# A float32 feed-forward down-projection by Strassen's scheme in four passes, tokens on the output's partitions

## The chip, the cores and the metric

The kernel runs on one core of a Trainium2 chip. What is measured is the device time of one execution, in microseconds (us). Five engines work side by side, each with its own queue in program order: TensorE (PE, matmuls), VectorE (DVE), ScalarE (ACT), GpSimd (POOL) and SyncE (SP, which here only starts transfers). SP, ACT and POOL each have a queue of DMA issues; all transfers share 16 DMA engines.

## The reference, cut to what matters

One layer of a streaming encoder, 512 tokens, width 2048, everything in float32: a token mixer, a cross-attention into 256 memory tokens, and a feed-forward part, each added to a residual, and a final RMSNorm. The change is about the end of it:

```python
def conv_ffn(h, w_up, conv_w, w_down):
    u = causal_dwconv(h @ w_up, conv_w)
    gate, up = u[..., :D_FF], u[..., D_FF:]
    return (jax.nn.silu(gate) * up) @ w_down
...
        x = x + conv_ffn(h, w_ffn_up[l], ffn_conv[l], w_ffn_down[l])
    return rmsnorm(x, final_norm)
```

D_FF is 5632, so the hidden matrix is 512 x 5632 and w_down is 5632 x 2048.

## The kernel before

Activations lie transposed, channels on the 128 partitions and the 512 tokens along the row. A float32 product is made of three matmuls of a rounded type: each operand is split into a high part (an ACT cast) and a low part (a DVE subtraction), and high x high, low x high and high x low are summed in PSUM (mm3, L153 to L156). Weights come in pieces of 128 x 1024 (512 KB): wpiece (L134 to L145) loads one on SP's queue into one of five buffers and splits it into one of three pairs of buffers, whi and wlo (L143, L144); raw and wsplit (L829 to L839) do the same in two steps. Small tiles of 128 x 512 come from a pool of 64 (T).

**Out-projection.** The loop at L860 makes 16 tiles of the residual: 24 matmuls each into a bank psx (out_proj), the old residual tile loaded on SP and added on DVE (L878), the sum stored to x2_d on ACT's queue (L879), its square added on POOL (L245), and after each second tile up_prepare makes, on DVE and ACT, the sums that the next stage needs.

**Up-projection.** The loop over 44 units (L953) makes a gate tile and an up tile of the hidden matrix by Strassen's scheme: seven products of 24 matmuls with 256 columns each (product, L898 to L900). pair_loads (L841) loads four weight pieces and lets two accumulating loads on POOL's queue make sums of them; the others are made on DVE. up_half (L946) and gate_half (L940) apply the norm, the convolution, Silu and the product of both, and L951 stores the tile to hid_d on ACT's queue.

**Down-projection.** The output is made transposed, four tiles of 128 channels at a time (four PSUM banks), over eleven steps of four hidden tiles. Steps run in the order of the list steps (L913): 44 of them, the last two of them held back. Each step loads four hidden tiles on POOL's queue (hid_load, L919), splits them (hid_split), loads and splits two weight pieces (w_split, two pieces ahead) and issues 48 matmuls of 512 columns; the hidden matrix is so loaded and split four times. At the end of a group the residual tile is added (L1075) and its square summed. The order on ACT, DVE and POOL is written out (manual_schedule, L1042), PE's is the scheduler's.

**End.** The last two steps run again by token halves (tail_mm, 256 columns, L1079), so that the norm of the first half can be made beside the second: rstd_rows (L231) sums squares over partitions on PE and rsqrt (L209) takes Ln and Exp on ACT and three DVE operations. out_pair (L1105) multiplies and stores on SP's queue (L1110); the host transposes the result.

## Time and profile before

| | us |
|---|---|
| median of 3 runs (2832.14 to 2836.43) | 2833.61 |
| the profiled execution | 2834.4 |
| its span, first to last instruction | 2832.6 |
| PE busy | 2806.2 |
| DVE busy | 1835.9 |
| ACT busy | 1354.3 |
| POOL busy | 351.9 |

The profile is one execution seen by the hardware profiler. Busy time of PE contains matmuls that overlap each other, so a busy share of 99% says that PE was never without one, not that it works at its peak. The duration of a matmul (0.389 us for 512 columns) is longer than the distance from one to the next. Where an engine was idle, the profile names what released it. The clock that TensorE was granted is 0.998 of full speed over the span.

### The profile page before, as it was taken

How to read it: one execution, taken by the hardware profiler on the slowest of the kernel's cores; microseconds unless marked ns; L12 is line 12 of the kernel's file. 1: busy time of each engine (PE TensorE's matmuls, PEld its weight loads, DVE VectorE, ACT ScalarE, POOL GpSimd, SP SyncE). 2: the span in 40 equal slices, each digit the busy share in tenths (PEclk: the TensorE clock that was granted, in tenths of full speed). 3: DMA queues.
4: the chain of work that ended last, by engine and by line, in shares of the span. 5: the costliest groups of instructions: out<-in, count | busy, mean ns of one | idle time of the engine just before them, and what ended most of it. 6: DMA issues, size and time to landing. Idle time of an engine off the chain costs nothing.

```text
span 2832.6 us, 44271 instructions
## 1 busy us (share of the span) xinstructions
PE 2806.2 (99%) x17581; PEld 2521.2 (89%) x17581; DVE 1835.9 (65%) x2713; ACT 1354.3 (48%) x1914; POOL 351.9 (12%) x425
## 2 busy tenths in 40 slices
PE   9999999999999999999999999999999999999997
PEld 9999878888788888888889999999999998888887
DVE  6456647877874334446688787878787875444445
ACT  6564644354443323235565555555555554434353
POOL 2110001021110000110110000000000012213130
PEclk9999999999999999999999999999999999999999
DMA  7785854333322224446566666666666667465562
GB/s 258 242 275 188 271 165 112 100 94 108 93 89 98 95 97 156 149 145 186 177 183 160 181 160 182 160 181 160 182 159 184 159 189 258 170 216 203 169 237 90
DMA packets 178943, 472.92 MB, mean 167 GB/s; under 512 B 26656, under 2 KB 50608, under 8 KB 178736
## 3 DMA queue, kind: packets, MB, share of 16 engines
q1 hardware_dynamic: 131040, 335.31, 36.1%
q0 software_dynamic: 29840, 102.27, 15.7%
q10 hardware_dynamic: 17856, 32.51, 3.0%
q8 instruction: 137, 2.24, 0.3%
q14 instruction: 70, 0.57, 0.1%
HBM read 425.97 MB, written 44.06 MB: 166 GB/s over the span
## 4 chain that ended last, share of the span: by engine, by line
PE 70%; DVE 1%; ACT 0%; issue 0%; POOLq 0%; DVEq 0%; ACTq 0%
PE px L898 6%; PE px L899 6%; PE px L900 6%; PE psd L154 6%; PE psd L155 6%; PE psd L156 6%; PE pssc L154 3%; PE psx L155 3%; PE psx L156 3%; PE psx L154 3%; PE pssc L156 3%; PE pssc L155 3%; PE pz L900 3%; PE pz L899 3%; PE pz L898 3%; PE py L898 1%
## 5 line engine op out<-in xcount | busy, mean ns | idle before, releaser
L144 DVE TENSOR_TENSOR wlo<-wst,whi 128x1024 fp32r<-128x1024 f32 x400 | 493.8, 1235 | 547.5 <-ACT whi L143 546.2
L143 ACT CAST whi<-wst 128x1024 fp32r<-128x1024 f32 x400 | 420.2, 1051 | 766.9 <-PE psd L155 214.5
L837 ACT CAST whi<-wst 128x1024 fp32r<-128x1024 f32 x177 | 185.5, 1048 | 290.3 <-PE px L899 143.2
L898 PE MATMUL px<-xoh,whi 128*128 128x256 f32 x1056 | 299.2, 283 | 2.3 <-ACT tq L965 1.4
L900 PE MATMUL px<-xoh,wlo 128*128 128x256 f32 x1056 | 298.8, 283 | 0.0
L899 PE MATMUL px<-xol,whi 128*128 128x256 f32 x1056 | 298.8, 283 | 0.0
L838 DVE TENSOR_TENSOR wlo<-wst,whi 128x1024 fp32r<-128x1024 f32 x177 | 217.3, 1228 | 95.9 <-ACT whi L837 57.9
L154 PE MATMUL psd<-hdh,whi 128*128 128x512 f32 x672 | 261.4, 389 | 0.0
L155 PE MATMUL psd<-hdl,whi 128*128 128x512 f32 x672 | 261.4, 389 | 0.0
L156 PE MATMUL psd<-hdh,wlo 128*128 128x512 f32 x672 | 261.4, 389 | 0.0
L898 PEld LDWEIGHTS px<-xoh,whi 128*128 128x128 f32 x1056 | 202.7, 192 | 2.9 <-ACT tq L965 1.8
L899 PEld LDWEIGHTS px<-xol,whi 128*128 128x128 f32 x1056 | 202.7, 192 | 0.0
L900 PEld LDWEIGHTS px<-xoh,wlo 128*128 128x128 f32 x1056 | 202.7, 192 | 0.0
L900 PE MATMUL pz<-xoh,wlo 128*128 128x256 f32 x704 | 199.4, 283 | 0.9 <-DVE wlo L838 0.9
L898 PE MATMUL pz<-xoh,whi 128*128 128x256 f32 x704 | 199.2, 283 | 0.0
L899 PE MATMUL pz<-xol,whi 128*128 128x256 f32 x704 | 199.2, 283 | 0.0
L837 ACT CAST whi<-s 128x1024 fp32r<-128x1024 f32 x131 | 137.2, 1048 | 88.3 <-PE px L899 61.7
L838 DVE TENSOR_TENSOR wlo<-s,whi 128x1024 fp32r<-128x1024 f32 x131 | 160.3, 1223 | 1.9 <-ACT whi L837 1.9
L154 PE MATMUL psq<-hh,whi 128*128 128x512 f32 x384 | 155.9, 406 | 0.0
L154 PE MATMUL pssc<-hh,whi 128*128 128x512 f32 x384 | 153.2, 399 | 0.0
L156 PE MATMUL psq<-hh,wlo 128*128 128x512 f32 x384 | 150.1, 391 | 0.0
L155 PE MATMUL psq<-hl,whi 128*128 128x512 f32 x384 | 150.0, 391 | 0.0
(340 smaller groups left out, 7394.6 us busy)
## 6 DMA issues: line engine op xcount, KB each, us to landing
wst<-in_w_up SPq DMA_DIRECT2D x132, 512.0 KB, 4.7
wst<-in_w_mix SPq DMA_DIRECT2D x112, 512.0 KB, 3.5
wst<-in_w_dn SPq DMA_DIRECT2D x88, 512.0 KB, 3.5
hid<-hid_d POOLq DMA_DIRECT2D x176, 256.0 KB, 4.7
s<-in_w_up POOLq DMA_DIRECT2D x87, 512.0 KB, 6.6
s<-in_w_up SPq DMA_DIRECT2D x43, 512.0 KB, 4.9
wst<-in_w_xq SPq DMA_DIRECT2D x32, 512.0 KB, 4.8
wst<-in_w_xv SPq DMA_DIRECT2D x32, 512.0 KB, 3.5
```

The lines of the kernel that those rows point to most:

```text
L143: nc.scalar.copy(hi, st)
L144: nc.vector.tensor_tensor(lo, st, f(hi), op=ALU.subtract)
L154: nc.tensor.matmul(ps, wh, xh, start=first, stop=False)
L155: nc.tensor.matmul(ps, wh, xl, start=False, stop=False)
L156: nc.tensor.matmul(ps, wl, xh, start=False, stop=last)
L837: nc.scalar.copy(hi, t)
L838: nc.vector.tensor_tensor(lo, t, f(hi), op=ALU.subtract)
L898: nc.tensor.matmul(ps, hi[:, c], xh, start=first and k == 0, stop=False, skip_group_check=True)
L899: nc.tensor.matmul(ps, hi[:, c], xl, start=False, stop=False, skip_group_check=True)
L900: nc.tensor.matmul(ps, lo[:, c], xh, start=False, stop=k == HK - 1, skip_group_check=True)
```

## The change

**The scheme.** The hidden matrix is cut into two halves of tokens and two halves of D_FF (22 tiles each), w_down into two halves of D_FF and two of output channels, and the down-projection is made of seven products of halves with sums of halves. Tokens are now on the output's partitions: the hidden matrix is the operand whose 128 columns are loaded, a weight row of 1024 channels is the one that streams through, as two times 512 columns. One product fills four PSUM banks (two tiles of tokens, two of channels), 22 rows long. Passes one to three run two products side by side (eight banks), pass four one. The list slots has one entry for each row of each product; for each, rows issues 12 matmuls.

**Hidden sums.** Units of the up-projection are taken in pairs k and k + 22 (up_order). Behind the second one, four DVE operations of 256 columns make the four sums of halves, and seven half tiles (128 x 256) are stored to hf_d, 1 KB rows, in four transfers on ACT's queue. The passes load them as pairs, one 256 KB tile a row (every second row in pass four), on SP's queue, three rows ahead (fac_load), and split them one or two rows ahead (fac_split).

**Weight sums.** make(i + 2) prepares the weights two slots ahead. Per row, the first pass loads two blocks of 512 KB, the second one, the third two, and the fourth one for each second row. Sums of weights are made on DVE, in halves of 512: two subtractions a row in passes one and two (kept in the tiles store, 22 x 512 KB), two additions a row in pass three, and two each second row in pass four; the other 11 rows of pass four get their last block by accumulating loads on POOL's queue (add_block, seven in pass three, four in pass four).

**Combination.** Finished banks are copied by ACT (passes one and two) or added by DVE (L1075's place) into c11, c12, p7 and u2, four tiles of 128 x 512 each; single steps of that are put into a list later and taken one per slot. The residual is added by accumulating loads on POOL's queue (add_rest).

**Residual.** Because tokens are now on partitions, each residual tile is transposed on PE (turn_rest, four transposes of 128 x 128 into one bank), copied by ACT into one buffer and stored to x2t_d in pieces of 512 bytes on ACT's queue. That happens in the middle of the next tile's product; the order of PE in this loop is now written out. The tile pool tb has eight buffers in place of seven and is closed one unit later.

**End.** Sums of squares are taken along the row by ACT's squares, so PE sums nothing over partitions. The first 256 tokens are normed and stored during pass four. The last two rows of pass four run bank by bank, each bank's sum and square behind it; then comes the second factor and eight output tiles. POOL adds no squares in this stage any more. The final gain is loaded as a row (fin). The result leaves in its final layout.

```diff
-    x2_d = dpool.tile([KT, P, S], F32, tag="x2_d", name="x2_d")
-    hid_d = dpool.tile([NF, P, S], F32, tag="hid_d", name="hid_d")
+    x2t_d = dpool.tile([4, P, D], F32, tag="x2t_d", name="x2t_d")
+    hf_d = dpool.tile([NF // 2, 7, P, S // 2], F32, tag="hf_d", name="hf_d")
...
+    KD = NF // 2
+    up_order = [pos // 2 + pos % 2 * KD for pos in range(NF)]
...
+    def turn_rest():
+
+        if turned:
+            n, x1 = turned.pop()
+            psT = PG("psxt")
+            for j in range(4):
+                nc.tensor.transpose(v4(psT)[:, j], v4(x1)[:, j], ident)
+            x2t = cpool.tile([P, S], F32, tag="macc", name=nm("x2t"))
+            nc.scalar.copy(x2t, psT)
+            nc.scalar.dma_start(x2t_d[:, :, n * P : (n + 1) * P].rearrange("j p c -> p j c"), v4(x2t))
...
+            out_proj(0)
+            turn_rest()
+            out_proj(1)
...
+            turned.append((n, x1))
...
-    def hid_load(i):
-        if i < len(steps):
-            raws[i] = [T("hid") for _ in range(FC)]
-            for k in range(FC):
-                nc.gpsimd.dma_start(raws[i][k], hid_d[steps[i][1] * FC + k])
...
+    A11, NS2, A12 = 2, 3, 5
+    phases = ((0, 2), (2, 4), (4, 6), (6, 7))
+    slots = [(ph, k, j) for ph in range(3) for k in range(KD) for j in range(2)] + [(3, k, 0) for k in range(KD)]
+    store, pieces, fac, fraw, held = {}, {}, {}, {}, {}
+    adding = list(range(0, KD, 2))
+
+    def fkey(ph, k):
+        return (ph, k // 2 * 2) if ph == 3 else (ph, k)
...
+    def fac_load(ph, k):
+        if (ph, k) == fkey(ph, k) and (ph, k) not in fraw:
+            fraw[ph, k] = T("hid")
+            src = hf_d[k : k + 2, 6] if ph == 3 else hf_d[k, phases[ph][0] : phases[ph][1]]
+            nc.sync.dma_start(fraw[ph, k].rearrange("p (f s) -> p f s", f=2), src.rearrange("f p s -> p f s"))
+
+    def fac_split(ph, k):
+        if (ph, k) == fkey(ph, k) and (ph, k) not in fac:
+            fac_load(ph, k)
+            fac[ph, k] = split(fraw[ph, k], "hd")
...
+    def sum_parts(ts):
+        hi = wp.tile([P, 1024], F32R, tag="whi", name=nm("whi"))
+        lo = wp.tile([P, 1024], F32R, tag="wlo", name=nm("wlo"))
+        n = 1024 // len(ts)
+        for i, t in enumerate(ts):
+            nc.scalar.copy(hi[:, i * n : (i + 1) * n], t)
+        for i, t in enumerate(ts):
+            sl = slice(i * n, (i + 1) * n)
+            tt(lo[:, sl], t, f(hi)[:, sl], op=ALU.subtract)
+        return hi, lo
...
+        ph, k, j = slots[i]
+        if ph == 0 and j == 0:
+            held[0] = block(1, 1, k)
+            ts = [held[0]]
+        elif ph == 0:
+            t = block(0, 1, k)
+            store[k] = halves(US("store")) if k >= KD - 4 else [T("store") for _ in range(2)]
+            for dst, x, y in zip(store[k], halves(t), halves(held[0])):
+                tt(dst, x, y, op=ALU.subtract)
+            ts = store[k]
+        elif ph == 1 and j == 0:
+            held[0] = block(0, 0, k)
+            ts = [held[0]]
+        elif ph == 1:
+            for dst, y in zip(store[k], halves(held[0])):
+                tt(dst, dst, y, op=ALU.subtract)
+            ts = store[k]
+        elif ph == 2 and j == 0:
+            t = block(1, 1, k)
+            for x, y in zip(halves(t), store[k]):
+                tt(x, x, y, op=ALU.add)
+            ts = [t]
+        elif ph == 2:
+            ts = [block(1, 0, k)]
+            if k % 3 == 2:
+                add_block()
+        elif k % 2 == 0:
+            ts = store[k]
+        else:
+            t = block(1, 0, k)
+            for x, y in zip(halves(t), store[k]):
+                tt(x, x, y, op=ALU.add)
+            ts = [t]
+        pieces[i] = sum_parts(ts)
+
+    def add_block():
+
+        if adding:
+            k = adding.pop(0)
+            for dst, src in zip(store[k], halves(g["w_dn"][KD + k, 0])):
+                nc.gpsimd.dma_start(dst, src, accum_op=ALU.add)
...
+        if pos % 2 == 0:
+            h1[:] = [cpool.tile([P, S], F32, tag="macc", name=nm("h1"))]
+            tt(h1[0], gate, cv, op=ALU.mult)
+            nc.scalar.dma_start(hf_d[k, 2], h1[0][:, LO])
+            return
         tt(gate, gate, cv, op=ALU.mult)
-        nc.scalar.dma_start(hid_d[i], gate)
+        s21 = cpool.tile([P, 2, NMEM], F32, tag="rmem", name=nm("s21"))
+        s43 = cpool.tile([P, S], F32, tag="xacc", name=nm("s43"))
+        a, b = h1[0], gate
+        tt(s21[:, 1], a[:, HI], b[:, HI], op=ALU.add)
+        tt(s21[:, 0], a[:, LO], s21[:, 1], op=ALU.subtract)
+        tt(s43[:, HI], a[:, HI], a[:, LO], op=ALU.subtract)
+        tt(s43[:, LO], b[:, LO], s21[:, 0], op=ALU.add)
+        nc.scalar.dma_start(hf_d[k, 3:5].rearrange("f p s -> p f s"), s21)
+        nc.scalar.dma_start(hf_d[k, 0:2].rearrange("f p s -> p f s"), s43.rearrange("p (f s) -> p f s", f=2))
+        nc.scalar.dma_start(hf_d[k, 5:7].rearrange("f p s -> p f s"), b.rearrange("p (f s) -> p f s", f=2))
...
+        turn_rest()
...
+    def banks(second):
+        if second:
+            return [PG("psd") for _ in range(4)]
+        return [PM("psd") for _ in range(3)] + [PG("psd")]
+
+    def rows(bs, w, xs, off, first, last, only=None):
+        hi, lo = w
+        xh, xl = xs
+        for b in range(4) if only is None else (only,):
+            t, ns = b // 2, b % 2
+            c = slice(off + t * P, off + (t + 1) * P)
+            n = slice(ns * S, (ns + 1) * S)
+            mm3_(bs[b], xh[:, c], xl[:, c], hi[:, n], lo[:, n], first, last)
+
+    def mm3_(ps, xh, xl, wh, wl, first, last):
+        nc.tensor.matmul(ps, xh, wh, start=first, stop=False)
+        nc.tensor.matmul(ps, xl, wh, start=False, stop=False)
+        nc.tensor.matmul(ps, xh, wl, start=False, stop=last)
...
+    def factor(ss, s2):
+
+        tot = sp.tile([P, 2], F32, tag="tot", name=nm("tot"))
+        nc.vector.tensor_reduce(tot, ss.rearrange("p (j m) -> p j m", j=2), axis=AX.X, op=ALU.add)
+        ms = sp.tile([P, 2], F32, tag="ms2", name=nm("ms2"))
+        return rstd(tot, ms)
+
+    def out_tile(src, j, m, r):
+        o = T("o")
+        nc.vector.scalar_tensor_tensor(o, src, r[:, j % 2 : j % 2 + 1], gain[m], op0=ALU.mult, op1=ALU.mult)
+        nc.sync.dma_start(g["out"][j][:, m * S : (m + 1) * S], o)
...
+        for i, (ph, k, j) in enumerate(slots):
+            if k == 0 and j == 0:
+                bs = [banks(q) for q in range(1 if ph == 3 else 2)]
+            a = ph * KD + k
+            for dist, act in ((3, fac_load), (2 if ph == 3 else 1, fac_split)):
+                if a + dist < 4 * KD:
+                    act((a + dist) // KD, (a + dist) % KD)
+            make(i + 2)
+            if ph == 3 and k % 2 == 0:
+                add_block()
+            if later and k > 0:
+                later.pop(0)()
+            if ph == 3 and k == KD - 2:
+                continue
+            if ph == 3 and k == KD - 1:
+                break
+            rows(bs[j], pieces.pop(i), fac[fkey(ph, k)], (k % 2 if ph == 3 else j) * S2, k == 0, k == KD - 1)
+            if k < KD - 1:
+                continue
+            if ph == 0 and j == 0:
+                c12 = quad("c12")
+                for c, b in zip(c12, bs[0]):
+                    nc.scalar.copy(c, b)
...
+                for q in range(4):
+                    later.append(lambda q=q: add_rest(c12[q], q // 2, 2 + q % 2))
...
+                u2 = quad("u2")
+                for u, c, b in zip(u2, c11, bs[1]):
+                    tt(u, c, b, op=ALU.add)
+                for q in range(4):
+                    later.append(lambda q=q: tt(c12[q], c12[q], u2[q], op=ALU.add))
+                    later.append(lambda q=q: tt(p7[q], p7[q], u2[q], op=ALU.add))
+                for q in range(4):
+                    later.append(lambda q=q: add_rest(c11[q], q // 2, q % 2))
+            elif ph == 2 and j == 0:
+                for q in range(4):
+                    tt(c12[q], c12[q], bs[0][q], op=ALU.add)
+                    tt(u2[q], p7[q], bs[0][q], op=ALU.add)
+            elif ph == 2:
+                for q in range(4):
+                    tt(c11[q], c11[q], bs[1][q], op=ALU.add)
+                ss01 = sp.tile([P, 8], F32, tag="ss01", name="ss01")
+                ss23 = sp.tile([P, 8], F32, tag="ss23", name="ss23")
+                gain, r = [], []
+                for q in range(4):
+                    add_rest(u2[q], 2 + q // 2, 2 + q % 2)
+                for q in range(4):
+                    add_rest(p7[q], 2 + q // 2, q % 2)
...
+                for q in range(4):
+                    later.append(lambda q=q: square(c11[q], ss01, q // 2 * 4 + q % 2))
+                    later.append(lambda q=q: square(c12[q], ss01, q // 2 * 4 + 2 + q % 2))
+                later[3:3] = [gains]
+                later.append(lambda: r.append(factor(ss01, "a")))
+                for q in range(4):
+                    later.append(lambda q=q: (out_tile(c11[q], q // 2, q % 2, r[0]), square(u2[q], ss23, q // 2 * 4 + 2 + q % 2)))
+                    later.append(lambda q=q: (out_tile(c12[q], q // 2, 2 + q % 2, r[0]), tt(u2[q], u2[q], gain[2 + q % 2], op=ALU.mult)))
+        for n_, run in enumerate(later):
+            run()
+        nc.scalar.activation(cst[:, 3:4], cst[:, 0:1], AF.Ln)
+        n = len(slots)
+        for q in range(4):
+            for i in (n - 2, n - 1):
+                rows(bs[0], pieces[i], fac[fkey(3, KD - 2)], (i - n + 2) * S2, False, i == n - 1, only=q)
+            tt(p7[q], p7[q], bs[0][q], op=ALU.add)
+            square(p7[q], ss23, q // 2 * 4 + q % 2)
+        rb = factor(ss23, "b")
+        for q in range(4):
+            j, m = 2 + q // 2, q % 2
+            out_tile(p7[q], j, m, rb)
+            o = T("o")
+            nc.scalar.activation(o, u2[q], AF.Identity, scale=rb[:, q // 2 : q // 2 + 1])
+            nc.sync.dma_start(g["out"][j][:, (2 + m) * S : (3 + m) * S], o)
```

## Rows read from the trace of the kernel before

**Rows 1.** The profile's page, parts 1, 2 and 4: busy times, transfers by slice, chain.
```profile
PE 2806.2 (99%) x17581; PEld 2521.2 (89%) x17581; DVE 1835.9 (65%) x2713; ACT 1354.3 (48%) x1914; POOL 351.9 (12%) x425
...
DMA  7785854333322224446566666666666667465562
GB/s 258 242 275 188 271 165 112 100 94 108 93 89 98 95 97 156 149 145 186 177 183 160 181 160 182 160 181 160 182 159 184 159 189 258 170 216 203 169 237 90
...
PE 70%; DVE 1%; ACT 0%; issue 0%; POOLq 0%; DVEq 0%; ACTq 0%
```

**Rows 2.** By stretch, tiles psd: length; busy us (instructions) PE, PEld, DVE; clock; DMA share; GB/s.
```profile
2335.70:2792.40 456.70, 456.70 (x2015) 378.18 (x2016) 9.69 (x15) 1.00 0.58 200
2792.40:2816.50 24.10, 23.59 (x194) 23.30 (x193) 3.64 (x8) 1.00 0.14 47
```

**Rows 3.** Timeline of ACT, down-projection: start, us, instruction, idle before and what ended it.
```profile
2439.04 1.05 ACT L143 CAST whi<-wst 128x1024 fp32r<-128x1024 f32 x1 [3.35 <-PE psd L155]
2440.00 1.14 ACT L149 CAST hdh<-hid 128x512 fp32r<-128x512 f32 x2
```

**Rows 4.** Timeline of DVE, the same stretch.
```profile
2440.13 1.23 DVE L144 TENSOR_TENSOR wlo<-wst,whi 128x1024 fp32r<-128x1024 f32 x1 [3.01 <-ACT whi L143]
2441.27 1.29 DVE L150 TENSOR_TENSOR hdl<-hid,hdh 128x512 fp32r<-128x512 f32 x2
...
2453.36 1.88 DVE L1075 TENSOR_TENSOR x<-psd,x 128x512 f32<-128x512 f32 x3
```

**Rows 5.** The same, all instructions: PE, PEld, DVE, ACT, POOL; out-, up- and down-projection.
```profile
1360.00:1445.00 85.00, 85.00 (x383) 70.63 (x383) 60.37 (x94) 49.45 (x79) 19.57 (x16) 1.00 0.59 180
1500.00:2300.00 800.00, 800.00 (x6669) 800.00 (x6668) 652.64 (x795) 440.81 (x557) 67.90 (x79) 1.00 0.65 171
2340.00:2790.00 450.00, 450.00 (x1987) 372.61 (x1986) 220.94 (x280) 197.96 (x301) 107.49 (x181) 1.00 0.58 199
```

**Rows 6.** The chain that ended last, 1354 to 1358: four transposes between two matmuls.
```profile
1357.02 0.44 PE ppt L739 x4
```

**Rows 7.** Timeline of all engines in the out-projection, 1383 to 1392.
```profile
1383.40 1.05 ACT L143 CAST whi<-wst 128x1024 fp32r<-128x1024 f32 x1 [0.86 <-PE psx L155]
...
1386.84 0.68 DVE L878 TENSOR_TENSOR x<-psx,x 128x512 f32<-128x512 f32 x1
...
1387.55 0.33 ACTq L879 DMA_DIRECT2D x_d<-x  x1
...
1391.30 0.68 DVE L878 TENSOR_TENSOR x<-psx,x 128x512 f32<-128x512 f32 x1
```

**Rows 8.** Timeline of all engines behind the last matmul, 2816.5 to the end.
```profile
2816.74 0.42 DVE L1093 TENSOR_TENSOR x<-psd,x 128x256 f32<-128x256 f32 x1
...
2819.08 0.47 ACT L219 ACTIVATE rsy<-psn,cst 128x256 f32<-128x256 f32 x1 [1.06 <-DVE ms L228]
2819.57 1.28 ACT L220 ACT_TABLE_LOAD   x1
...
2822.76 4.91 DVE L1109 TENSOR_TENSOR o<-o,rsy 128x512 f32<-128x512 f32 x8
```

**Rows 9.** Groups by line and shape, 1280 to 1480: busy us, mean ns, idle before.
```profile
L772 ACT ACTIVATION_READ_ACCUMULATOR pr<-pss,mx,rs 128x1 f32 x16 | 3.4, 214 | 0.0
L767 DVE TENSOR_SCALAR mx<-mx,nrs 128x2 f32<-128x2 f32 x8 | 1.4, 222 | 0.0
...
L937 DVE SCALAR_TENSOR_TENSOR ucv<-ug,cols,ucv 128x511 f32<-128x511 f32 x1 | 0.7, 743 | 0.0
```

**Rows 10.** DMA issues by line: count, KB of one, median us from issue to landing.
```profile
wst<-in_w_dn SPq DMA_DIRECT2D x88, 512.0 KB, 3.5
...
mo_d<-mo ACTq DMA_DIRECT2D x32, 256.0 KB, 5.9
...
wst<-mo_d SPq DMA_DIRECT2D x16, 512.0 KB, 4.1
...
x_d<-x ACTq DMA_DIRECT2D x16, 256.0 KB, 4.2
```

More of the change, by code (lines that the diff above doesn't have):

```diff
@@ L900, in product @@
             nc.tensor.matmul(ps, lo[:, c], xh, start=False, stop=k == HK - 1, skip_group_check=True)
-    NC_ = NF // FC
-    GN = 4
-    acc3 = cpool.tile([P, S], F32, tag="macc", name="acc3")
-    x3 = []
-    def bank(gq, q):
-        return (PG if q < 2 or (q == 3 and gq % 2 == 0) else PM)("psd")
-    steps = [(gq, c) for gq in range(KT // GN) for c in range(NC_)]
-    raws, parts_, ws = {}, {}, {}
-    def hid_load(i):
-        if i < len(steps):
-            raws[i] = [T("hid") for _ in range(FC)]
-            for k in range(FC):
-                nc.gpsimd.dma_start(raws[i][k], hid_d[steps[i][1] * FC + k])
@@ new lines, in block, with halves @@
+    def block(r, c, k):
+        return raw(g["w_dn"][r * KD + k, c])
+    def halves(t):
+        return [t[:, :S], t[:, S:]]
+    def sum_parts(ts):
[8 more added lines that the diff above has]
+        return hi, lo
@@ new lines, in make @@
+    def make(i):
+        if i >= len(slots) or i in pieces:
+            return
[33 more added lines that the diff above has]
+        pieces[i] = sum_parts(ts)
@@ new lines, in quad @@
+    def quad(s2):
+        return [T(s2) for _ in range(4)]
+    def banks(second):
[10 more added lines that the diff above has]
+            mm3_(bs[b], xh[:, c], xl[:, c], hi[:, n], lo[:, n], first, last)
```

222 lines of the change are left out of this document (67 added, 155 removed).

## The prediction

> **What bounds the kernel now.** I read the page's busy times and its chain of waits first [rows 1]: PE is busy for 99% of the span, and the chain runs over PE's matmuls. So time is won by fewer matmuls, as long as their operands keep coming. Then the down-projection itself: its 2016 full matmuls (512 columns) start one after another over 456.7 us, 0.2265 us each, and its 192 half ones (256 columns) take 24.1 us with the sums of squares between them [rows 2]. Together 480.8 us without a gap, at full clock. Last, who has room there. ACT rounds a weight block when PE gives a buffer free (3.35 us idle until PE's matmul), DVE subtracts behind it (3.01 us idle until ACT) [rows 3, 4], and over 450 us DVE is busy for 221 us, ACT for 198 [rows 5]. Two facts for the sums: instructions of one engine overlap their ends. Two 512-wide ACT casts take 1.14 us, three 512-wide DVE additions 1.88, two subtractions 1.29 [rows 3, 4], so one more costs ACT 0.52 and DVE 0.60; a 1024-wide subtraction costs 1.14 (2440.13 to 2441.27), all of its 1.23 only where something waits for it. A cast of 1024 takes 1.05 and hands over in 0.04.
>
> **Matmuls.** The old work is 2112 full ones (2016 and 192 halves). The new one has 154 slots (three passes of 22 block rows with two products, one pass with one), each with four banks of three matmuls, 1848 in all, with as many columns and one weight load each as before. 1848 x 0.2265 = 418.6 us in place of 480.8: **-62.2**.
>
> **Residual turned.** Sixteen times four transposes are new on PE, in the out-projection, where PE is never idle [rows 5]. The same transposes stand in the chain with 0.44 us for four [rows 6]: 16 x 0.44 = **+7.0**. The order of PE is now written out, so the turn stands 12 matmuls (2.72 us) behind the end of the tile's product and PE waits there if the residual sum is late. One product ended at about 1383.5 (the cast at 1383.40 was held by it), the next 24 x 0.2265 = 5.4 later. Their sums ended at 1387.5 and 1392.0, 4.0 and 3.0 us behind the products' ends [rows 7]: 1.3 and 0.3 us too late in turn, 15 x 0.8 = 12 us if DVE's order stays; 0 if the sum goes ahead of the two subtractions before it. DVE's order is left to the scheduler here, and a longer slot lets those subtractions end earlier: I take the middle, **+6** (0 to 12). ACT copies each turned tile (about 0.6; a 512-wide cast is of that size), with room: 49 of 85 us busy. The copy's single buffer waits for the previous store; that is a rival below. SP gets the same loads here, POOL nothing.
>
> **Up-projection.** A pair of units gets four 256-wide operations more on DVE (4 x 0.42 = 1.7 us in 40) and two stores more on ACT's queue. DVE idles 147 of 800 us there [rows 5], 3.7 us per unit of 168 matmuls or 20.2 us. Weights are made two products (5.8 us) ahead. I cost it at 0. If that cover were gone it would be 22 x 1.7 = 37 us. At the handover, the last unit's DVE chain is longer by the same 1.7 us, while a slot is now half as long: **+1** (0 to 2).
>
> **First and second pass.** A block row gives PE 24 x 0.2265 = 5.44 us and DVE one 1024-wide subtraction and five 512-wide operations, 1.14 + 5 x 0.60 = 4.1. Nothing waits. Copies out of the banks are ACT's, which spends about 2.7 of 5.44.
>
> **Third pass.** Now DVE first adds twice, ACT can cast only then, DVE waits: 0.60 (units' low part) + 0.60 + 0.69 + 0.04 + 1.05 + 0.04 + 1.14 + 1.14 = 5.3 of 5.44 us. No room is left for what is put in between: four sums at the end of the second pass (2.4 us) and eight more in the first eight slots (4.8). Three weight buffers let DVE run about 2 slots ahead, of which some 2 to 3 us can be lost before PE waits; about 0.5 us a row fits into gaps. **+3.5** (0 to 8).
>
> **Fourth pass.** A pair of slots gives PE 5.44 us and DVE 3 x 0.60 = 1.8 on the even row, 0.60 + 0.69 + 1.05 + 1.14 + 0.08 = 3.56 on the odd one: 5.36, again no room. On top, in DVE's written order: twelve sums out of the banks at the third pass's end (7.2); the first rows' factor, where DVE waits for ACT: two table loads of 1.28 [rows 8], and four small DVE and two small ACT operations of about 0.2 (0.22 in the row of two columns), some 3.5; eight output tiles (0.66 each, an operation of 0.74) and four multiplications, 7.7. Squares with a sum add 0.21 on ACT; these small rows are [rows 9], 0.6 us in all for the DVE operations behind them. Of these 19.0 us the lead takes 3. And the last two slots now run bank by bank, so PE needs the last weights after 6 matmuls of slot 20 instead of 12: 2.0 more. **+18** (8, if the lead and gaps take more; 22 with nothing hidden).
>
> A rule of the Trainium skill against this term: "ScalarE: Activation LUTs", section "Table sets: the hidden batching unit", has logarithm and exponential in one set, with one load. By it the factor would be 1.3 us shorter here and at the end. The rows differ: a load of 1.28 stands between Ln and Exp of the same factor [rows 8], and I keep two.
>
> **End.** The last sum out of PE starts at 2816.74, the last of eight output tiles ends at 2827.67, the span at 2832.6 [rows 8]: 16.2 us behind the last matmul (2816.4). New: sum 0.69, square 0.84, small operations and one load between them 2.8, four tiles on DVE 2.7 (four more on ACT beside them), the same 4.9 for the last store: 11.9. **-4.3** (-6 to -2).
>
> **Transfers at nothing.** Each pass reads no more per time than has been seen but the third (below). Factors are loaded three block rows ahead (16 us) against 3.5 to 5.9 us for landing [rows 10]. SP takes 3 loads per row, each well below 1 us of its queue; loads no longer wait behind POOL.
>
> **Sum.** The profiled execution took 2834.4 us (span 2832.6), 0.8 above the median of the runs: -62.2 + 7.0 + 6 + 1 + 3.5 + 18 - 4.3 = -31, so **2803.4 us**. With all low ends -62.2 + 7 + 8 - 6 = -53 (2781), with all high ones -62.2 + 7 + 12 + 2 + 8 + 22 - 2 = -13 (2821).
>
> **Rivals.**
> 1. *DVE never holds PE.* If the two-slot lead swallows the passes' extras: -62.2 + 7.0 + 6 - 4.3 = -53.5, 2781. For: DVE is at 49% now. Against: the chain through ACT in rows three and four, worked out above, has no room. 0.12.
> 2. *Transfers hold the third pass.* At 0.58 of the DMA engines 199 GB/s go now, 343 GB/s at all of them; in the up-projection 0.65 carry 171 GB/s, of which 117 are plain (four loads of 512 KB and a store of 256 KB per 20.15 us, 0.34 of the engines). So two accumulating loads of 512 KB take 0.31 x 20.15 = 6.2 us, 3.1 each, twice a plain one [rows 5]. The third pass moves 22 x 1.31 MB (84 us of all engines), seven accumulated blocks (22) and four residual tiles (6): 112 of 119.6 us, 0.94. The busiest slice of the kernel shows 8 tenths at 275 GB/s [rows 1]. If 0.8 is what it gets, the pass takes 140 us: +20, less the 3.5 that it covers: 2820. Against: buffers are five deep, and nothing shows that 0.8 is a limit. 0.17.
> 3. *The turned residual's store is slow: slower than before.* The copy has one buffer, written again after the store's landing. Copy 0.6, issue 0.33 and landing L must fit into a slot of 5.9 us: L up to 4.9 costs nothing. ACT is in order, so beyond that each tile costs the excess, with the rounding of weights behind it. Stores of the residual in 2 KB rows land in 4.2 us, the other store on ACT's queue in 5.9 [rows 10]: 15 x 1.0, 2818. The forecast is used up at L = 7.0, 31/15 = 2.1 more; at twice today's 4.2 it is 15 x 3.5 = 52, 2856. For it: pieces are 512 bytes now in place of 2 KB. Against: loads in 512-byte pieces of 512 KB land in 4.1 us against 3.5 in long rows. 0.08. "Perfetto Trace Analysis", section "DMA Optimizations", of the Trainium skill says that transfers in pieces under 2 KB pay much for each; by it this rival is likelier. The 4.1 against 3.5 shows some of that, though no factor of two.
>
> That the change does less than it says is no case here: the matmul count follows from its loops.
>
> **Chances and range.** Forecast 0.58, rivals 0.12, 0.17 and 0.08, other waits on either side 0.05. About 0.2% (5.7 us) is what a measurement of this kernel can tell from none. Faster by more: the forecast, rivals 1 and 2 nearly whole, 0.88; within it, 0.03; slower 0.09. The range runs from all low ends and rival 1 to just above rival 2 and the milder form of rival 3: 2781 to 2825.
>
> **What would show it.** The matmuls of the output stage: 1848 at 0.2265 us. PE idle until DVE's low part of weights: a few us early in the third pass, most of 18 in the fourth, first at its start and again from its middle. Waits of the transposes on the residual sum, below 1 us each. ACT's copies of turned tiles never held by a store. The forecast is wrong if PE idles on DMA in the third pass, if it has no idle time in the fourth, or if the out-projection grows by more than 20 us.

## The result and the profile after

The changed kernel takes 2819.49 us (median of 4 runs, 2817.63 to 2820.14) against 2834.01 for the kernel before in the same session: ratio 0.9947, 95% interval 0.993 to 0.9964. It is faster by 14.5 us, where the forecast had 31 (2803.4 against the profiled 2834.4). The profiled execution took 2817.63 us, its span is 2815.7. The page's busy times answer to [rows 1]: PE has 39 us less to do and is idle for 48.5 us of the span, where it was idle for 26.4.

```profile
PE 2767.2 (98%) x17277; PEld 2474.9 (88%) x17277; DVE 1983.0 (70%) x2979; ACT 1379.9 (49%) x1944; POOL 267.2 (9%) x258
```

The four passes of the down-projection in the changed kernel, by stretch, tiles psd, with the columns of [rows 2] (ACT has a column too). They start at 2343.63, where the kernel before started at 2335.70 [rows 2].

```profile
2343.63:2466.20 122.57, 120.33 (x528) 98.97 (x529) 0.00 (x0) 3.33 (x7) 1.00 0.73 247
2466.20:2585.89 119.69, 119.69 (x530) 99.10 (x529) 0.00 (x0) 3.10 (x7) 1.00 0.50 155
2585.89:2712.56 126.67, 123.39 (x529) 99.74 (x528) 5.19 (x9) 0.00 (x0) 0.99 0.86 261
2712.56:2802.41 89.85, 71.13 (x265) 51.38 (x263) 6.70 (x11) 0.00 (x0) 0.92 0.55 144
```

At 0.2265 us a matmul the passes would take 119.6, 119.6, 119.6 and 59.8 us. So the first loses 2.9, the second nothing, the third 7 and the fourth 30. The waits of the fourth pass, 2712 to 2803 (engine, tile and line, what it waited for; us in total, times, longest):

```profile
PE psd L1132 <- ACT whi L955: 14.7, 9, 3.3
DVE wlo L958 <- ACT whi L955: 13.4, 11, 1.3
...
ACT hdh L149 <- DMA hid<-hf_d: 10.5, 3, 5.4
...
PE psd L1134 <- DVE wlo L958: 3.7, 8, 0.5
```

PE waits for split weights, as forecast, though mostly for ACT's high part (14.7 us) and only 3.7 us for DVE's low part, which the forecast had named. And behind ACT stands a wait that the forecast did not have: 10.5 us for the down-projection's factors (hid, the tiles of the hidden matrix that are multiplied by the weights), which ACT rounds ahead of the next weights. ACT's timeline there:

```profile
2731.00 0.62 ACT L149 CAST hdh<-hid 128x512 fp32r<-128x512 f32 x1 [5.38 <-DMA hid<-hf_d]
...
2747.26 0.62 ACT L149 CAST hdh<-hid 128x512 fp32r<-128x512 f32 x1 [4.77 <-DMA hid<-hf_d]
```

What else was on the way then is seen in POOL's timeline at the third pass's end. The residual's eight tiles for u2 and p7 and the first five halves of blocks leave its queue within 12.5 us; three more halves and four gain loads follow until 2738.

```profile
2711.64 1.83 POOL L1137 DMA_DIRECT2D u<-x2t_d  x2 [54.46 <-PE psd L1134]
...
2715.76 3.87 POOL L1137 DMA_DIRECT2D p<-x2t_d  x4
2717.91 6.26 POOL L1005 DMA_DIRECT2D store<-in_w_dn  x5
```

and in the DMA issues of 2712 to 2762 (KB of one, median us to landing):

```profile
store<-in_w_dn POOLq DMA_DIRECT2D x8, 256.0 KB, 14.4
hid<-hf_d SPq DMA_DIRECT2D x6, 256.0 KB, 7.6
...
p<-x2t_d POOLq DMA_DIRECT2D x4, 256.0 KB, 10.8
```

The factor that ACT waited for until 2731.00 was issued at 2718.79. ACT was ready for it 6.8 us later (2725.62), but its landing took 12.2 us (SP's timeline, and the DMA issues of 2715 to 2722):

```profile
2718.79 0.50 SPq L937 DMA_DIRECT2D hid<-hf_d  x1
...
hid<-hf_d SPq DMA_DIRECT2D x1, 256.0 KB, 12.2
```

The DMA engines are full (a share of 1.07 to 1.11), and TensorE pays twice: it idles, and then runs slowly. By stretch, all instructions (columns: PE, PEld, DVE, ACT, POOL; clock; DMA share; GB/s):

```profile
2720.00:2730.00 10.00, 7.63 (x29) 4.77 (x27) 5.01 (x8) 1.67 (x3) 5.46 (x7) 1.00 1.08 216
2730.00:2740.00 10.00, 7.81 (x23) 6.14 (x24) 6.79 (x11) 5.62 (x11) 3.38 (x5) 0.66 1.10 273
...
2730.00:2732.00 2.00, 0.00 (x0) 0.00 (x0) 0.35 (x1) 1.00 (x2) 0.56 (x1) 0.72 1.07 305
...
2732.00:2736.00 4.00, 3.81 (x9) 2.93 (x10) 2.76 (x6) 2.37 (x6) 1.08 (x3) 0.50 1.11 240
```

TensorE waited 3.3 us for a rounded weight, to 2732. The granted clock behind that is 0.50 (1.2 GHz in place of 2.4) in each microsecond from 2732 to 2737. Five at half speed lose some 2.5 us more (an estimate from that clock).

### The profile page after: what moved, and what is told of

It is laid out like the page before. It is cut to its first block, busy times and chain, and to the rows that moved or that the text cites. A ratio compares the mean times of both kernels' runs of the same rounds, so it can differ in the third digit from the quotient of the medians.

```text
span 2815.7 us, 43966 instructions
## 1 busy us (share of the span) xinstructions
PE 2767.2 (98%) x17277; PEld 2474.9 (88%) x17277; DVE 1983.0 (70%) x2979; ACT 1379.9 (49%) x1944; POOL 267.2 (9%) x258
## 4 chain that ended last, share of the span: by engine, by line
PE 65%; DVE 2%; DMA 1%; ACT 1%; issue 1%; SPq 0%; DVEq 0%; ACTq 0%
PE px L916 6%; PE px L917 6%; PE px L918 6%; PE psd L1134 4%; PE psd L1132 4%; PE psd L1133 4%; PE pssc L154 3%; PE pssc L156 3%; PE pssc L155 3%; PE psx L155 3%; PE psx L154 3%; PE psx L156 3%; PE pz L918 3%; PE pz L916 3%; PE pz L917 3%; PE py L918 1%
## 5 line engine op out<-in xcount | busy, mean ns | idle before, releaser
L144 DVE TENSOR_TENSOR wlo<-wst,whi 128x1024 fp32r<-128x1024 f32 x316 | 389.5, 1234 | 328.4 <-ACT whi L143 326.8
L143 ACT CAST whi<-wst 128x1024 fp32r<-128x1024 f32 x316 | 331.7, 1050 | 554.6 <-PE pssc L155 143.8
L837 ACT CAST whi<-wst 128x1024 fp32r<-128x1024 f32 x177 | 185.6, 1049 | 271.4 <-PE px L917 143.5
L838 DVE TENSOR_TENSOR wlo<-wst,whi 128x1024 fp32r<-128x1024 f32 x177 | 216.4, 1223 | 70.3 <-ACT whi L837 68.9
L1132 PE MATMUL psd<-whi,hdh 128*128 128x512 f32 x616 | 244.5, 397 | 17.3 <-ACT whi L955 15.8
L1134 PE MATMUL psd<-wlo,hdh 128*128 128x512 f32 x616 | 244.1, 396 | 6.8 <-DVE wlo L958 6.7
L1133 PE MATMUL psd<-whi,hdl 128*128 128x512 f32 x616 | 243.0, 394 | 0.2 <-DVE hdl L150 0.2
L958 DVE TENSOR_TENSOR wlo<-wst,whi 128x1024 fp32r<-128x1024 f32 x99 | 119.8, 1224 | 76.9 <-ACT whi L955 76.3
L955 ACT CAST whi<-wst 128x1024 fp32r<-128x1024 f32 x99 | 102.0, 1050 | 135.9 <-DVE wst L985 50.0
L1132 PEld LDWEIGHTS psd<-whi,hdh 128*128 128x128 f32 x616 | 117.4, 191 | 46.4 <-ACT whi L955 21.1
```

The lines of the kernel that those rows point to most:

```text
L143: nc.scalar.copy(hi, st)
L144: nc.vector.tensor_tensor(lo, st, f(hi), op=ALU.subtract)
L837: nc.scalar.copy(hi, t)
L838: nc.vector.tensor_tensor(lo, t, f(hi), op=ALU.subtract)
L1132: nc.tensor.matmul(ps, xh, wh, start=first, stop=False)
L1133: nc.tensor.matmul(ps, xl, wh, start=False, stop=False)
```

## The experiments

The theory: the residual's accumulating loads, the blocks and the gains start close together at the third pass's end, and hold the factors' loads; this costs the fourth pass some 12 of its 30 us. The rival: VectorE's written order makes all 30. "Pass" times are from the first matmul of a pass to that of the next, in the profiled execution of each run (a slot is 12 matmuls, 2.72 us). They are the better measure of a change here: in the twelve kernels that have the changed kernel's order up to there, the first matmul of the down-projection falls anywhere from 2342.1 to 2349.1 us. A unit is the 128 x 1024 of weights that one slot needs; "the blocks" are the accumulating loads (add_block) that complete units of the fourth pass. Each median is of 4 to 11 executions; the ratio is to the kernel before on the same chip.

| run | median us | ratio (95%) | third pass | fourth pass |
|---|---|---|---|---|
| changed kernel | 2819.49 | 0.9947 (0.993 to 0.9964) | 126.7 | 89.9 |
| x1_spread | 2818.67 | 0.9949 (0.9936 to 0.9961) | 126.7 | 90.2 |
| x2_norest | 2807.92 | 0.9911 (0.9897 to 0.9924) | 126.7 | 79.6 |
| x3_cover3 | 2815.10 | 0.9931 (0.9918 to 0.9945) | 124.1 | 90.2 |
| x4_cover4 | 2813.69 | 0.9927 (0.9915 to 0.994) | 126.7 | 85.6 |
| x5_gated | 2813.61 | 0.9934 (0.9922 to 0.9947) | 126.7 | 86.3 |
| x6_lead | 2809.05 | 0.9912 (0.9898 to 0.9925) | 126.7 | 79.7 |
| x7_turn | 2839.11 | 1.0021 (1.0012 to 1.003) | 126.7 | 90.0 |
| x8_tail | 2814.36 | 0.9935 (0.9923 to 0.9948) | 126.7 | 86.6 |
| z1_plain | 2814.46 | 0.9934 (0.9922 to 0.9947) | 126.7 | 86.4 |
| y1_joined | 2796.75 | 0.9873 (0.9858 to 0.9888) | 124.4 | 70.9 |
| y2_gaps | 2792.67 | 0.9858 (0.9842 to 0.9875) | 127.8 | 60.8 |
| y3_gated | 2783.57 | 0.9825 (0.9811 to 0.9838) | 120.9 | 62.0 |

**x1_spread.** The loads moved to later slots of the program:

```diff
-                for q in range(4):
-                    add_rest(u2[q], 2 + q // 2, 2 + q % 2)
...
+                spread = {1 + 2 * q: [lambda q=q: add_rest(u2[q], 2 + q // 2, 2 + q % 2)] for q in range(4)}
...
```

> Complete kernel: the changed kernel, with the residual's eight accumulating loads of the fourth pass issued one by one (those of u2 in slots 1, 3, 5, 7, those of p7 in slots 10, 12, 14, 16) and the four gain loads in slots 8 and 9, instead of all at the third pass's end. Theory (the transfers that start together at the third pass's end hold the factors' loads, and these the fourth pass): the two waits of ScalarE on a factor's load of some 5 us go, the DMA share between 8 and 28 us behind the third pass's end falls from 1.1 to under 0.9, the fourth pass falls from 89.9 to 77 to 80 us, the clock stays at its upper level there; whole kernel 10 to 12 us below the changed one, some 2808 us. Rival (the written order of VectorE alone makes the fourth pass's 30 us): the pass stays within 2 us of 89.9, the kernel at 2819.

A miss: 90.2 us, and ACT still waits 10.6 us for factors. But it does not speak for the rival, since the loads were not spread. POOL's timeline of this run:

```profile
2712.89 2.08 POOL L1005 DMA_DIRECT2D store<-in_w_dn  x2
2713.96 1.88 POOL L1137 DMA_DIRECT2D u<-x2t_d  x1
2714.50 3.11 POOL L1005 DMA_DIRECT2D store<-in_w_dn  x2
```

A slot of the program is no time for a queue that waits for nothing in it: POOL had issued the loads of slots 0 to 7 by 2719, six microseconds into the pass. Only p7's were later, behind the gain loads, which waited for tile buffers.

**x2_norest.** The eight loads behind the third pass are left out.

```diff
-                for q in range(4):
-                    add_rest(u2[q], 2 + q // 2, 2 + q % 2)
-                for q in range(4):
-                    add_rest(p7[q], 2 + q // 2, q % 2)
```

> Leaves out the residual's eight accumulating loads of the fourth pass (half of the output lacks its residual); blocks and gains stay where they are. Theory of the transfers: at least what the spread gives, the fourth pass 76 to 79 us, the kernel some 2807 us; what is left of the pass above 59.8 us is VectorE's order and the end. Rival (VectorE's order alone): 89.9 us for the pass, 2819 for the kernel. A third reading: if the four blocks alone can fill the queues, the pass keeps one wait on a factor of about 3 us, and the spread kernel is no worse than this one.

The pass falls by 10.3 us to 79.6, the wait on factors to 0.7:

```profile
ACT hdh L149 <- DMA hid<-hf_d: 0.7, 1, 0.7
```

So these loads cost 10 us. 20 us above 59.8 are left; x4, x8, y1 and y2 below show how much of them is VectorE's order and the last slots.

**x6_lead.** The same question from the other side, all loads left in place:

```diff
-            for dist, act in ((3, fac_load), (2 if ph == 3 else 1, fac_split)):
+            for dist, act in ((7 if a + 7 >= 3 * KD else 3, fac_load), (3, fac_load), (2 if ph == 3 else 1, fac_split)):
```

> Complete kernel: the factors of the fourth pass are loaded seven rows ahead in place of three, all else as in the changed kernel (its loads still start together). If the factors' lateness alone is what holds the fourth pass: waits on factors go, the pass falls to 80 us, the kernel to some 2810. If the loads of units and blocks are held as long behind the same transfers: ScalarE and VectorE wait for a unit's block instead, the pass falls by less than 5 us, the kernel stays above 2814. The rival of VectorE's order alone: 89.9 and 2819.

The pass falls to 79.7, as without the loads. No wait for a factor is left, while the DMA engines are as full as before. By stretch, all instructions:

```profile
2730.00:2740.00 10.00, 10.00 (x46) 8.05 (x45) 7.50 (x11) 6.63 (x13) 3.40 (x6) 1.00 1.10 266
2740.00:2750.00 10.00, 10.00 (x45) 8.06 (x44) 7.51 (x12) 6.73 (x15) 0.00 (x0) 1.00 1.07 329
```

TensorE is busy for all of both stretches at 2.4 GHz, beside a DMA share of 1.1, and in the whole pass neither ACT nor DVE waits for a load. Full DMA engines cost nothing in these 20 us; a load with too short a lead did. That settles 10 of the 30 us, and against the rival.

**x5_gated.** The spread of x1, with a real wait:

```diff
+                def gated(dst, j, m):
+                    nc.scalar.copy(dst[:, :1], dst[:, :1])
+                    add_rest(dst, j, m)
...
```

> Complete kernel: the spread of the first run again, but each accumulating load of the fourth pass now waits for a one-column copy on ScalarE in its slot (blocks in slots 1, 5, 9, 13; u2 in 2, 3, 6, 7; p7 in 10, 11, 14, 15; gains in 4 and 8), since GpSimd's queue ran ahead of the slots in the first run and the loads of u2 and the blocks left together all the same. Theory (loads that start together hold the factors): no wait of ScalarE on a factor above 2 us, the DMA share under 0.9 in every 10 us behind 2720, the pass at 79 to 82 us (the run without those loads had 79.6), the kernel 8 to 10 us below the changed one, some 2810. Rival (it is the bytes of these loads, wherever they are put): the pass stays above 86 us, the kernel above 2816.

A miss by the theory's own terms: 86.3 us, where it said 79 to 82 and the rival above 86; the kernel, 2813.61, lies between the two. The waits on factors are 6.2 us in four, the longest 2.5, and the DMA share is still 1.04 from 2730 to 2740 (all instructions, columns as above):

```profile
2730.00:2740.00 10.00, 9.81 (x41) 7.17 (x40) 6.01 (x9) 5.20 (x12) 2.82 (x4) 1.00 1.04 269
```

Spreading the same bytes makes the factors less late, but leads are what they were. That the bytes cost time wherever they are put is not the reason: x6 has all of them, and no such wait.

**z1_plain.** The eight loads without the sum:

```diff
+                def plain_rest(dst, j, m):
+                    nc.gpsimd.dma_start(dst, x2t_d[j, :, m * S : (m + 1) * S])
...
-                    add_rest(u2[q], 2 + q // 2, 2 + q % 2)
+                    plain_rest(u2[q], 2 + q // 2, 2 + q % 2)
...
```

> The changed kernel with the residual's eight loads of the fourth pass as plain loads over the tile, not accumulating ones: it leaves out those sums' first terms (half of the output is not the reference's), bytes, queue and time of issue are the same. If accumulating makes these loads long (the queue of accumulating loads took 0.23 of all engines' time per MB in the worst 22 us, the other queue 0.15): the fourth pass falls from 89.9 to 84 to 87 us, the kernel to some 2815. If it is only bytes that start together: 89 to 91 us, 2819.

86.4 us, in the range of the theory: with the same bytes and the same place in the same queue, plain loads cost the pass 3.5 us less. Waits on factors are 7.5 us in place of 10.5 (5.9 before the rounding of factors, 1.6 before that of weights behind them). The time of issue is not quite the same, though: POOL issues p7's four in 2.12 us in place of 3.87, so what comes behind them leaves sooner too (POOL's timeline below). How the 3.5 us divide between the transfers and the issuing stays open.

```profile
2715.25 2.12 POOL L1209 DMA_DIRECT2D p<-x2t_d  x4
```

**x3_cover3.** VectorE's order in the third pass. The sums go where VectorE waits for ScalarE:

```diff
         for i, t in enumerate(ts):
             nc.scalar.copy(hi[:, i * n : (i + 1) * n], t)
+        for run in mid:
+            run()
...
-                    later.append(lambda q=q: tt(c12[q], c12[q], u2[q], op=ALU.add))
-                    later.append(lambda q=q: tt(p7[q], p7[q], u2[q], op=ALU.add))
+                    mids.append(lambda q=q: tt(c12[q], c12[q], u2[q], op=ALU.add))
+                    mids.append(lambda q=q: tt(p7[q], p7[q], u2[q], op=ALU.add))
...
```

> Complete kernel: the eight sums of u2 into c12 and p7 in the third pass are written between a unit's rounding on ScalarE and its remainder on VectorE (where VectorE idles 1.25 us a row), two per row, in place of one per slot behind them. Theory (VectorE's written order has no room but that gap): the slots of 3.47, 2.94, 3.67, 2.95 and 3.68 us fall to 2.72 to 2.8, the third pass from 126.7 to 123 to 124 us, the kernel 3 us below the changed one, some 2816.5. Rival (VectorE is slowed there by the transfers and GpSimd's queue): slots stay long, 2819.

124.1 us, as expected: the eight sums cost 2.6 us by their place alone. VectorE's timeline has them in the gap, with no idle time shown before the remainders (L960); the last line belongs to what is told below it:

```profile
2600.14 0.69 DVE L1196 TENSOR_TENSOR c<-c,u 128x512 f32<-128x512 f32 x1
2600.75 0.69 DVE L1197 TENSOR_TENSOR p<-p,u 128x512 f32<-128x512 f32 x1
2601.48 2.36 DVE L960 TENSOR_TENSOR wlo<-wst,whi 128x1024 fp32r<-128x1024 f32 x2
...
2616.20 1.29 DVE L987 TENSOR_TENSOR wst<-wst,store 128x512 f32<-128x512 f32 x2 [0.93 <-DMA wst<-in_w_dn]
```

What stays above 2.72 us are the slots behind the four sums at the second pass's end (4.03 and 3.65) and slots 98 to 100, counted from 0 over all passes (3.59, 3.01, 3.66), where VectorE and ScalarE wait 2.1 us for units' loads. By the waits these are the transfers again: c11's residual leaves POOL's queue at 2601.35, four in a row. No run changes that alone.

**x4_cover4.** The same for the fourth pass's output tiles of c11 and the multiplications of u2 by the gain (in this run u2's squares are taken behind that multiplication, so half of the rows get another factor):

```diff
...
-                    later.append(lambda q=q: (out_tile(c11[q], q // 2, q % 2, r[0]), square(u2[q], ss23, q // 2 * 4 + 2 + q % 2)))
-                    later.append(lambda q=q: (out_tile(c12[q], q // 2, 2 + q % 2, r[0]), tt(u2[q], u2[q], gain[2 + q % 2], op=ALU.mult)))
+                    mids.append(lambda q=q: out_tile(c11[q], q // 2, q % 2, r[0]))
+                    mids.append(lambda q=q: tt(u2[q], u2[q], gain[2 + q % 2], op=ALU.mult))
+                    later.append(lambda q=q: square(u2[q], ss23, q // 2 * 4 + 2 + q % 2))
+                    later.append(lambda q=q: out_tile(c12[q], q // 2, 2 + q % 2, r[0]))
```

> Complete kernel: in the fourth pass the four output tiles of c11 and the four multiplications of u2 by the gain are written into the same gap (between rounding and remainder of the odd units), those of c12 stay. Theory (VectorE's order sets the pace there, with 1.2 us of idle time in each pair of slots): pairs fall from 7.4 to 6.1 to 6.3 us, four of them, the pass by 4 to 5 us to some 85 us, the kernel to some 2815. Rival (the pace is set by ScalarE or by the units' loads): pairs stay at 7.4, 2819.

85.6 us. A pair of slots takes 6.3 to 6.4 us in place of 7.3 to 7.4. What is above 5.44 fits the tiles of c12, left outside the gap: in y2, with all twelve operations inside, a pair takes 5.5.

**x8_tail.** The last two slots in slot order:

```diff
-            if ph == 3 and k == KD - 2:
-                continue
...
-            for i in (n - 2, n - 1):
-                rows(bs[0], pieces[i], fac[fkey(3, KD - 2)], (i - n + 2) * S2, False, i == n - 1, only=q)
+            rows(bs[0], pieces[n - 1], fac[fkey(3, KD - 2)], S2, False, True, only=q)
```

> Complete kernel: the last two slots are multiplied one after the other like all others, not bank by bank. Theory (bank by bank TensorE needs the last unit after 6 matmuls, and VectorE is late with it): the last two slots fall from 7.84 and 2.89 us to 3.7 and 4.0, 2.5 to 3 us; the last four sums then follow at 0.84 us (square) instead of 1.36, and end some 0.7 us further behind the last matmul: 2 us below the changed kernel, 2817.5. Rival (the bank order pays for itself in the end): 2819.5 or above.

The pass is 3.2 us shorter, with 3.72 and 3.82 us for the last two slots. The end behind the last matmul did not grow (13.3 us in both). The four sums now follow each other without a gap, 2.75 us together, where bank by bank each waited for TensorE. The bank order brought nothing.

**x7_turn.** One part of the change undone:

```diff
-            out_proj(0)
             turn_rest()
+            out_proj(0)
             out_proj(1)
```

> Complete kernel, one part undone: the residual's turn stands directly behind the tile's product in TensorE's order, not half a tile later. In the changed kernel the sums end 0.7 us or more behind the product and TensorE waited 0.7 us in all on them. Theory (half a tile of matmuls, 2.72 us, covers the sum): now TensorE waits in each of 15 turns for the end of the sum, 0.8 to 2.7 us each, the first matmul of the output stage comes 12 to 40 us later and so does the kernel's end: 2831 to 2859. Rival (the sum would be early in any order, the place of the turn is without effect): under 3 us.

The waits of this run, the transposes' line:

```profile
PE psxt L870 <- DVE x L897: 17.5, 15, 2.3
```

The changed kernel has one wait of 0.7 us there. Each of 15 turns now waits, 1.2 us on average; the output stage starts 23.6 us later, and the gain of the whole change is gone (ratio 1.0021). Half a tile of matmuls is worth 20 us.

**y1_joined.** x3, x4 (with the squares in their place), x6 and x8 together.

> Complete kernel: four changes measured alone are joined: factors of the fourth pass loaded seven rows ahead (its pass was 10.2 us shorter), the third pass's eight sums in the gap between rounding and remainder (2.6), output tiles of the fourth pass in that gap (here the eight tiles in pairs, the multiplications by the gain behind the squares; 4.3 in its run with four tiles and four multiplications), last two slots in slot order (3.3). Theory (four separate costs, each held by another wait): they add up, the third pass 124.1 us, the fourth 72 to 73, first matmul to last 439; the kernel 19 to 22 us below the changed one, some 2798. Rival (they are partly one cost, VectorE's lag, that any of them works off): the sum falls short by over 5 us, the kernel above 2803.

Third pass 124.4, fourth 70.9, 22.7 us below the changed kernel. The alone measured parts of the fourth pass, 10.2 + 4.3 + 3.2 = 17.7, are 19.0 together: separate costs.

**y2_gaps.** The sums out of the banks are taken off VectorE's path:

```diff
...
-                    tt(c12[q], c12[q], bs[0][q], op=ALU.add)
-                    tt(u2[q], p7[q], bs[0][q], op=ALU.add)
+                    nc.scalar.copy(u2[q], bs[0][q])
+                    mids.append(lambda q=q: tt(c12[q], c12[q], u2[q], op=ALU.add))
...
```

> Complete kernel: as the joined one, and besides the four sums at the second pass's end and the twelve at the third's are taken off VectorE's path: ScalarE copies the banks of the second pass's second product and of the third's first one (eight copies of 0.6 us), the sums follow two at a time in the gap between rounding and remainder of later units; the residual of c11 is loaded piece by piece, each waiting for a one-column copy on ScalarE; the fourth pass's residual loads follow their sums; the factor of the first rows is split in two slots, so that VectorE does not wait for ScalarE's two table loads. Theory (what is left above 59.8 us in the fourth pass and 119.7 in the third is the sums in VectorE's order and the factor): the third pass 120 to 122 us, the fourth 62 to 66, the kernel 8 to 14 us below the joined one, some 2787. Rival (the gaps are no room: ScalarE's copies or the transfers take their place): within 3 us of the joined one.

The fourth pass takes 60.8 us of 59.8: 29 of its 30 us are gone. The third, though, was expected at 120 to 122 and grew to 127.8, by one pause near its end, and the kernel is only 4.1 us below the joined one. POOL's and VectorE's timelines:

```profile
2667.59 6.48 POOL L1007 DMA_DIRECT2D store<-in_w_dn  x7
...
2691.11 1.29 DVE L987 TENSOR_TENSOR wst<-wst,store 128x512 f32<-128x512 f32 x2 [6.13 <-DMA wst<-in_w_dn]
```

The blocks had stood behind the residual's loads on POOL's queue. With those moved back they ran ahead into the third pass, seven together, and a unit's load came 6 us late. It looks like the mechanism of the fourth pass, in the third; the next run tests it.

**y3_gated.** Each of the fourth pass's blocks waits for one-column copies:

```diff
-            if ph == 3 and k % 2 == 0:
+            if ph == 3 and k in (0, 3, 6, 9):
+                for t in store[adding[0]]:
+                    nc.scalar.copy(t[:, :1], t[:, :1])
                 add_block()
```

> Complete kernel: the last one with one correction. There the third pass had one pause of 7 us near its end: the fourth pass's four block loads no longer stood behind the residual's loads on GpSimd's queue, ran ahead into the third pass (seven in a row at 2667 us, DMA share 1.0 to 1.1) and held the units' blocks. Now each waits for one-column copies on ScalarE in slots 0, 3, 6 and 9 of the fourth pass. Theory (loads that start together hold the units' blocks, in whatever pass they fall): the pause goes, the third pass 120 to 122 us, the fourth stays at 60 to 62, the kernel 5 to 7 us lower, some 2786. Rival (the pause has another cause, or the blocks now hold the fourth pass): 2790 or above.

The pause is gone. The passes of this kernel:

```profile
2342.75:2465.37 122.62, 120.38 (x529) 98.98 (x529) 0.00 (x0) 3.34 (x7) 1.00 0.73 247
2465.37:2585.05 119.68, 119.68 (x530) 99.13 (x528) 0.00 (x0) 3.21 (x8) 1.00 0.50 155
2585.05:2705.97 120.92, 120.39 (x529) 98.96 (x528) 0.00 (x0) 4.14 (x8) 1.00 0.90 279
2705.97:2767.96 61.99, 60.77 (x265) 48.95 (x263) 4.06 (x7) 0.00 (x0) 1.00 0.77 198
```

2783.57 us: 50 us below the kernel before and 36 below the changed one, with the full clock in all four passes. The interval of its ratio, 0.9811 to 0.9838, lies below that of the changed kernel.

## Why the prediction was half right

**Matmuls, right.** 1848 at 0.2265 us, as in the second pass (119.69 for 528).

**Residual turned, right with a smaller wait.** The down-projection starts 7.9 us later, where 13 were forecast. A turn costs 0.50 us and not 0.44: transposes follow each other at 5.94 us (1388.24, 1394.18), products at 5.44 before. The waits are 0.7 in place of 6, and the low end of the range was the true one: in the new kernel VectorE's sum waits for TensorE itself in seven turns, and it ends 0.7 to 2.0 us behind the product in 14 of 15. One of them:

```profile
1391.65 0.69 DVE L897 TENSOR_TENSOR x<-psx,x 128x512 f32<-128x512 f32 x1 [3.13 <-PE psx L156]
```

The working's lateness of 1.3 and 0.3 us was also read 0.4 too high: the cast at 1383.40 does not mark the product's end, which TensorE's own rows put at 1383.9. x7 shows what the place of the turn hides.

**Handover, +1 forecast, 2.9 measured.** TensorE waits 1.3 us until VectorE frees a bank in the up-projection's last chain (L1027), and again some slots on, for a low part:

```profile
PE psd L1132 <- DVE uu L1027: 1.3, 1, 1.3
PE psd L1134 <- DVE wlo L958: 1.0, 1, 1.0
```

Nothing was tried on it, its cause was only read, and it stays in y3.

**Third pass, +3.5 forecast, 7 measured.** The reason holds: no room in VectorE's order. By the runs 2.6 are the eight sums (x3). The other 4.5 are, by their slots, the four sums at the second pass's end and loads late behind c11's residual; y3 changes both together, and all but 1.3 of the seven are gone. Rival 2 (transfers hold this pass) is there in small: some 2 us in slots 98 to 100 against 20. Its 0.8 of the DMA engines is no limit: y3's third pass runs at 0.90.

**Fourth pass, +18 forecast, 30 measured.** Without late factors 19.8 are left (x2, x6): VectorE's share, near the 18. The total fits better than its parts. By the slots of x6, the first four lose 5.3 us (the twelve sums, 7.2 forecast less a lead of 3), the slot of the norm's factor 1.8 (3.5), the seven slots behind it 6.8 (7.7 and 0.6) and the last two 5.8 (2.0). Undone in runs, the bank order of the last two gives 3.2 (x8), eight of the twelve operations at the end 4.3 (x4), and the sums and the factor together 10.1 (y1 to y2, with the rest of the twelve operations).

**Transfers at nothing: the step that failed.** It said "Factors are loaded three block rows ahead (16 us) against 3.5 to 5.9 us for landing". That holds for the passes before: a row of the fourth pass is one slot, 2.72 us, not two, so that three rows are 8 us, and ScalarE rounds a factor one row behind its load; in the trace it was ready for it 6.8 us behind the issue. And the landing times were those of an even load: one factor's landing took 12.2 us here, where residual and blocks had left within 12.5. The text had itself put an accumulating 512 KB at 3.1 us of all engines; eight residual tiles of half that size and four blocks are some 25 us, which it set against whole passes, not against the few slots in which they are issued. It costs 10.2 us (x6), the lower clock behind the pauses among them. That is nearly the whole 12 by which the term was too small.

**End, -4.3 forecast, -2.8 measured** (13.3 us behind the passes' end at 2802.41, against 16.1 behind 2816.50 [rows 2], where the 480.8 us end).

**Rivals.** 1 (VectorE never holds TensorE) is wrong for this order of instructions, and nearly right for y3's: 62.0 us with the same number of operations on VectorE (2979) and twenty copies more on ScalarE, eight of whole banks and twelve of one column. 3 (the turned residual's store) fell: its stores land in a median of 3.2 us (DMA issues of 1360 to 1455), and a store held the copy once, for 1.3 us. In shorter pieces they are not slower than the 4.2 of [rows 10], though there beside other transfers:

```profile
x2t_d<-x2t ACTq DMA_DIRECT2D x15, 256.0 KB, 3.2
```

The rule of "Perfetto Trace Analysis", section "DMA Optimizations", of the Trainium skill, that small DMAs, under 2 KB, pay much for each transfer, is not seen when it is read of the 512-byte pieces of these 256 KB stores. The rule of "ScalarE: Activation LUTs", section "Table sets: the hidden batching unit", of the Trainium skill gave Ln and Exp one table; the changed kernel loads two, as forecast, in ACT's timeline at the norm factor of the first rows:

```profile
2759.90 1.28 ACT L219 ACT_TABLE_LOAD   x1
2761.20 0.30 ACT L219 ACTIVATE rsy<-tot,cst 128x2 f32<-128x2 f32 x1
2761.51 1.28 ACT L220 ACT_TABLE_LOAD   x1
```

Together, measured less forecast: -5.1 (turns) + 1.9 (handover) + 3.5 (third pass) + 12.1 (fourth) + 1.5 (end) = +13.9, which makes 2817.3 of the 2803.4; the profiled execution took 2817.63. That the miss is 14 us and not 19 is luck: the turns' waits, taken from the middle of 0 to 12, hid 5 of the 19 us by which the other terms were too low.

## What to carry to other kernels

Check a load's lead against the landing time at the worst moment, not the mean: list what leaves every queue in the few microseconds in which its neighbours are issued, and turn the lead into time of the stage in which it is used. To spread loads, give each something to wait for (a one-column copy); a queue that waits for nothing runs ahead of the program's slots, and taking one load out of its order lets those behind it go sooner. And where two engines hand a tile to and fro in written order, put the other work into the wait between the two halves: the same operations then cost next to nothing (60.8 us of 59.8 in y2's fourth pass).

## What the runs showed of the hardware

An accumulating load of 256 KB cost more than a plain one at the same place in the same queue: 3.5 us of the pass for eight, and four of them kept POOL's queue for 3.87 us in place of 2.12. A DMA share of 1.07 to 1.10 over 20 us left TensorE busy for all of it where its loads had been issued early (x6). And the 3.3 us pause in the changed kernel's fourth pass was followed by 5 us at a granted clock of 0.50: the late load was paid for nearly twice (3.3 and, by estimate, 2.5 us).
